# Attention's even-pair buffers over memory that the recurrence frees early, and a new order of the first loads and copies

## The chip, the cores and the metric

The kernel runs on one core of a Trainium2 chip. The metric is the device time of one execution in microseconds (us); the median of three runs is 3353.46 (3352.36 to 3354.02). Below, PE is TensorE (matrix multiplies), DVE is VectorE, ACT is ScalarE, POOL is GpSimd and SP is SyncE, which issues most of the transfers.

## What is computed

One layer over 2048 tokens of width 1024: a projection into many columns, a chunked attention branch, a recurrent branch, a gated merge, a residual, and a feed-forward network with a second residual.

```python
h   = RMSNorm_pre(x)
P   = h @ w_in            # q/k/v, r/k/v + low-rank w/a/g, branch gates
yA  = chunk-band attention (own chunk of 64 + 8 previous, bias on clipped distance)
yB  = RWKV-7 time mixing (token shift, decay, delta-rule state update over time)
m   = sigmoid(gA) * (yA @ proj_a) + sigmoid(gB) * (yB @ proj_b)
x   = x + RMSNorm_post(m @ w_out)
x   = x + RMSNorm_post2(relu(RMSNorm_pre2(x) @ w_up)^2 @ w_down)
```

## The kernel before, in words

**Arithmetic.** All products are of float32 precision made from three passes: each operand is split into a high part (a rounded copy, made by ACT) and a low part (the difference, made by DVE), and `mm3` (L78) multiplies high by high, high by low and low by high.

**Weights.** `wsplit` (L60 to L66) loads a block of 128 x 1024 (512 KB) into `wraw` from SP's queue, then ACT casts it into `whi` (L69) and DVE subtracts into `wlo` (L70). The pool `w` has two buffers of each, so the load of block n+2 waits for wlo of block n, and whi of block n+2 waits for the last matmul of block n. `dense` (L105) is one such block: 24 matmuls of 128 x 512 into `psd`.

**Stages.** The tokens are worked in four groups of 512. `phase_norm` (L313) makes the normed, transposed and split `hh`/`hl` of group 0: four tiles of 128 tokens, each loaded (x, L300), squared on ACT (L303), scaled on DVE with the broadcast gain g_pre (L306), and turned by PE (`pstr`, L144). Then each group runs

- `phase_rwkv`: dense blocks for the recurrence and the gates, and the recurrence of four pairs of heads, with `rwkv_pre` (L372) as the part ahead of each pair. `mix` (L325 to L329) takes a dense block's result, `lora` its low-rank parts, and E (L400) is the decay; X (L535) starts from x0, a pattern of ones spread over the partitions.
- `phase_attention`: four pairs (`att_pair`, L789). Each takes the old keys and values (KK, VV, L796 and L797) from memory, makes QA and QB from a dense block (L805 to L808; ACT and DVE in turn), then keys, values, scores and sums. `load_bias` (L902) reads the distance bias from `skew` in memory.
- `phase_merge`: four blocks of proj_b into md, four blocks of proj_a into th (`branches`, L961; the sum th + md, L978; its split into mh and ml, L69 and L70), then w_out in two halves (`ps_o`, L995), copied out by ACT (L1001). Beside it run the residual of the group before (o_prev L1024, transposed into `ps_ht` at L1030), and the norm of the next group (L300 to L306), or in the last group `combinations` (cmb, L1082) and the first operand of the feed-forward part (bh and bl, L1089 and L1090).

Then the feed-forward part runs in two halves.

**Constants.** `constants` (L150) is a generator. Its first part runs ahead of `phase_norm`, its second part behind: nine small loads into `rows` (L216), `raw2w` and `raw2a` (L223), `build_bias` (L236), which writes `band` (L896) and copies each of its eight rows of 768 over 128 partitions into `skew` (L898, eight transfers of 384 KB), and the x0 spread of eight transfers of 16 KB (L242).

**Order and memory.** A tile scheduler sets the order of the instructions on each engine; each engine then runs its own list in that order, with semaphores between them. Every pool is a stretch of SBUF; pools that open later reuse the addresses of pools that closed, and an instruction that writes there waits for the last users. Transfers from SP are also in order: one that waits holds back all behind it. In the attention, the pool `at` (two buffers, KK, VV, QA, QB among others) lies at 74400 to 135200 bytes of each partition and `atp` (PT, and the recurrence's output y) at 135200 to 176160.

Of the kernel before, what the change touches and what calls it, by code (L numbers as in the profile page):

```python
# [8 lines left out]
F32 = mybir.dt.float32  # L9
BF16 = mybir.dt.bfloat16  # L10
F32R = mybir.dt.float32r
# [6 lines left out]
P = 128  # L18
D = 1024
# [4 lines left out]
G = 512  # L24
GT = G // P
C = 64
# [14 lines left out]
RW0 = 1536  # L41
# [3 lines left out]
def advance(steps, n=None):  # L45

    while n is None or n > 0:
        if next(steps, steps) is steps:
            return
        n = n and n - 1  # L50


class Block:
# [3 lines left out]
        self.NG = self.S // G  # L57


    def wsplit(self, src, k, n):  # L60

        raw = self.wp.tile([P, k, n], F32, tag="raw", name="wraw")
        self.nc.sync.dma_start(raw, src)
        hi, lo = (self.wp.tile([P, k, n], F32R, tag="w" + x, name="w" + x) for x in ("hi", "lo"))
        self.split(hi, lo, raw)
        return hi, lo  # L66
# [41 lines left out]
    def dense(self, col):  # L108


        if self.g == 0:
            self.order.append(col)
            wh, wl = self.wsplit(*self.block(col))
        else:
            wh, wl = next(self.feed)
        ps = self.pd.tile([P, G], F32, tag="d", name="psd")
        self.mm = self.mm3(ps, [(wh[:, k], wl[:, k], self.h[0][:, k], self.h[1][:, k]) for k in range(KB)])
        return ps
# [31 lines left out]
    def constants(self, ctx, mixing):  # L150
        tc, nc, a = self.tc, self.nc, self.a
        keep = ctx.enter_context(tc.tile_pool(name="const", bufs=1))
        cp = mixing.enter_context(tc.tile_pool(name="mconst", bufs=1, side="right"))
        dp = ctx.enter_context(tc.tile_pool(name="scratch", bufs=1, space=DRAM))
# [50 lines left out]
        with tc.tile_pool(name="setup", bufs=1, side="right") as sp, \  # L205
             tc.tile_pool(name="setup_ps", bufs=1, space=PSUM, side="right") as pp:
            eye = sp.tile([2, 32, 16], F32, name="eye")
            nc.vector.memset(eye, 1.0)
            nc.gpsimd.affine_select(
                eye, eye, [[1, 32], [-2, 16]], ALU.is_equal, 0.0, base=0, channel_multiplier=-1  # L210
            )
            yield
            raw = sp.tile([nrow, P], F32, name="rows")
            at, off = 0, {}
            for name, n in rows:
                nc.sync.dma_start(raw[at : at + n], a[name].rearrange("(n p) -> n p", p=P))  # L216
                off[name] = at
                at += n
            raw2 = []
            for x in ("w2", "a2"):  # L220
                raw2.append(sp.tile([P, HW], F32, name="raw2"+x))
                for h in range(2):
                    nc.sync.dma_start(raw2[-1][h * C : h * C + C], a[x])  # L223
            ps = pp.tile([P, nrow], F32, name="ps_rows")
            nc.tensor.transpose(ps, raw, self.ident[:nrow, :nrow])
            nc.vector.tensor_copy(self.cst, ps)

            for par in range(2):
                r = slice(par * C, par * C + C)
                nc.scalar.copy(self.wh[par], raw2[par])  # L230
                o = slice(C - par * C, P - par * C)
                nc.vector.memset(self.wl[par][o].bitcast(F32), 0.0)
                nc.vector.tensor_tensor(
                    self.wl[par][r], raw2[par][r], self.wh[par][r].bitcast(F32), ALU.subtract
                )
            self.build_bias(sp, dp)  # L236
            eyeb = sp.tile([2, 512], BF16, name="eyeb")
            nc.vector.tensor_copy(eyeb, eye.rearrange("p r j -> p (r j)"))
            eyed = dp.tile([2, 512], BF16, name="eyed")
            nc.sync.dma_start(eyed, eyeb)  # L240
            for i in range(8):
                nc.sync.dma_start(  # L242
                    self.x0[i * 16 : i * 16 + 16].rearrange("p r j -> p (r j)"),
                    eyed[i % 2][None, :].to_broadcast((16, 512)),
                )

        def view(name, n):
            return self.cst[:, off[name] : off[name] + n]
# [44 lines left out]
        lo = self.hp.tile([P, KB, G], F32R, tag="hl", name="hl")  # L293
        return hi, lo

    def norm_steps(self, g, sp, pt, gt, t):

        nc = self.nc
        x = sp.tile([P, D], F32, tag="x", bufs=GT, name="x")
        nc.sync.dma_start(x, self.a["x"][g * G + t * P : g * G + (t + 1) * P])  # L300
        sq = sp.tile([P, D], F32, tag="sq", bufs=1, name="sqx")
        ssq = sp.tile([P, 1], F32, tag="ssq", bufs=4, name="ssq")
        nc.scalar.activation(sq, x, AF.Square, accum_out=ssq)  # L303
        r = self.rstd(sp, ssq, 1.0 / D, RMS_EPS)
        yield
        nc.vector.scalar_tensor_tensor(x, x, r, gt, op0=ALU.mult, op1=ALU.mult)  # L306
        yield
        if t == 0:
            self.h = self.alloc_h()
        self.transpose_split(pt, x, *self.h, slice(t * P, (t + 1) * P))  # L310
        yield

    def phase_norm(self, g, sp, pt):  # L313

        gt = self.gain(sp, self.a["pre_mix_g"], "g_pre")
        for t in range(GT):
            advance(self.norm_steps(g, sp, pt, gt, t))


    def mix(self, g, blk, out):  # L320
# [51 lines left out]
    def rwkv_pre(self, g, p, rp, NA, between=lambda: None):  # L372
        nc = self.nc
        pc = slice(p * P, (p + 1) * P)
        col = slice(p, p + 1)
# [8 lines left out]
        k = self.tmp("k")  # L384
# [5 lines left out]
        v = self.tmp("v")  # L390
        self.mix(g, 8 + p, v)

        between()
        nc.vector.tensor_scalar(tw, tw, -0.5 * DEC, -0.5 * DEC, ALU.mult, ALU.add)
        cum = tw
# [391 lines left out]


    def att_pair(self, g, p):  # L789
        nc, ap = self.nc, self.ap  # L790
        rows = [slice(0, C), slice(C, P)]
        first, lastg = g == 0, g == self.NG - 1
        KK = ap.tile([P, 2, 2, G], F32R, tag="KK", name="KK")
        VV = ap.tile([P, 2, GT, 2, C], F32, tag="VV", name="VV")
        if not first:
            nc.sync.dma_start(KK[:, :, 0].bitcast(F32), self.kc[p])  # L796
            nc.sync.dma_start(VV[:, 0], self.vc[p])  # L797
        bias = [self.load_bias(2 * p + par) for par in range(2)]

        ps = self.dense(ATT0 + p * P)  # L800
        QA = ap.tile([P, 2, G], F32R, tag="QA", name="QA")
        QB = ap.tile([P, 2, G], F32R, tag="QB", name="QB")
        for par in range(2):
            rw, ow = rows[par], rows[1 - par]
            nc.scalar.activation(QA[rw, par], ps[rw], AF.Copy, scale=-0.125)  # L805
# [79 lines left out]
    def build_bias(self, sp, dp):  # L885

        nc = self.nc

        self.skew = dp.tile([8, P * 769], F32, name="skew")
        band = dp.tile([8, 768], F32, name="band")  # L890
        ext = sp.tile([8, 768], F32, name="ext")
        nc.sync.dma_start(ext[:, 383:703], self.a["rel_rev"])
        nc.gpsimd.memset(ext[:, 703:768], 0.0)
        nc.vector.tensor_scalar(ext[:, 383:703], ext[:, 383:703], -1.0, None, ALU.mult)
        nc.vector.tensor_copy(ext[:, 0:383], ext[:, 383:384].to_broadcast((8, 383)))
        nc.sync.dma_start(band, ext)  # L896
        for h in range(8):
            nc.sync.dma_start(  # L898
                self.skew[h].rearrange("(q m) -> q m", m=769)[:, 0:768], band[h][None, :].to_broadcast((P, 768))
            )  # L900

    def load_bias(self, h):  # L902
        nc = self.nc
# [7 lines left out]
    def phase_attention(self, g):  # L911
        tc, nc = self.tc, self.nc
        self.yctx = ExitStack()
        yp = self.yctx.enter_context(tc.tile_pool(name="ya", bufs=1, side="right", reuse_waits="tile"))
        self.ya = self.alloc_y(yp)
        bp = self.yctx.enter_context(tc.tile_pool(name="br", bufs=1, side="right", reuse_waits="tile"))
        self.md = [bp.tile([P, 2, G], F32, name=f"md{i}") for i in range(KB // 2)]
        with ExitStack() as ctx:
            e = ctx.enter_context
            self.ap = e(tc.tile_pool(name="at", bufs=2, reuse_waits="tile"))  # L920
            pp = e(tc.tile_pool(name="atp", bufs=1, reuse_waits="tile"))
            self.psc = e(tc.tile_pool(name="atps", bufs=1, space=PSUM, reuse_waits="tile"))
            self.pt = e(tc.tile_pool(name="atpt", bufs=1, space=PSUM, reuse_waits="tile"))
            self.pv = e(tc.tile_pool(name="atpv", bufs=2, space=PSUM, reuse_waits="tile"))
            self.pts, self.npt = [], 0
            for i in range(2):
                self.pts.append([pp.tile([P, 6, 2 * P], F32, name=f"PT{par}{i}") for par in range(2)])
            for p in range(NP):
                self.att_pair(g, p)
                if p == 1:  # L930
                    for i in range(KB // 2):
                        self.load_gate(self.md[i], 1, i)
            y = self.load_y(pp, self.ap)
            for i in range(KB // 2):
                self.branches(y, self.md[i])
# [543 lines left out]
    def run(self):  # L1479
        tc, e = self.tc, None  # L1480
        with ExitStack() as ctx, ExitStack() as mixing:
            e = mixing.enter_context
            consts = self.constants(ctx, mixing)
            advance(consts, 1)
            self.pd = ctx.enter_context(tc.tile_pool(name="pd", bufs=2, space=PSUM))
            self.wp = e(tc.tile_pool(name="w", bufs=2))
            self.hp = e(tc.tile_pool(name="h", bufs=1))
# [82 lines left out]
```

## Time and profile before

| | |
|---|---|
| median of three runs | 3353.46 us |
| the profiled execution's own time | 3355.02 us |
| its span | 3353.1 us |
| PE busy | 3254.7 us, 97% |
| DVE busy | 2281.7 us, 68% |
| ACT busy | 1461.6 us, 44% |
| PE busy in the first 50 us | 29.19 us |

The span is what the profiler saw from the first to the last instruction. PE is at work for nearly all of it, so the idle time of PE is where to look; a wait of another engine costs only what PE waits for it. In the rows of a timeline, the first number is the start in us, the second the length, then engine, line, operation, output and inputs, count, and in brackets how long the engine had been idle and what released it. Rows of waits give the total in us, how many, and the longest.

### The profile page before, as it was taken

The numbers are of one execution on the slowest core, as the hardware profiler recorded it, in microseconds if no ns is written. First come the engines' busy times: TensorE is split into PE (matmuls) and PEld (weight loads), VectorE is DVE, ScalarE is ACT, GpSimd is POOL, SyncE is SP. The second block draws the span as 40 slices with busy tenths as digits, with TensorE's granted clock in tenths as the row PEclk, the third lists the DMA queues.
The fourth block names the chain that finished last, engine by engine and source line by source line (L and its number), as shares of the span: only waits on it lengthen the run. The fifth ranks groups of instructions, "written<-read, shape, count | busy, mean of one in ns | idle before, by whom it ended". The sixth has DMA issues, their size and how long they took to land. (4 is left out here: it accounts for less than half of the span.)

```text
span 3353.1 us, 49354 instructions
## 1 busy us (share of the span) xinstructions
PE 3254.7 (97%) x19089; PEld 2612.5 (78%) x19089; DVE 2281.7 (68%) x3806; ACT 1461.6 (44%) x2331; POOL 391.8 (12%) x732
## 2 busy tenths in 40 slices
PE   7999999999999999999999999999999999999998
PEld 5777777777777778777777777888887877888886
DVE  5774656675665774665774675876877777776778
ACT  3434634444644434644434644333331254454432
POOL 2110002110012210012210000111200011100002
PEclk9999999999999999999999999999999999999999
DMA  4224343125364224354224266334755364554443
GB/s 150 86 78 149 105 138 117 64 95 175 97 222 133 76 86 165 107 203 151 83 82 152 86 216 228 131 115 141 269 174 200 109 240 162 171 169 154 148 154 126
DMA packets 164945, 478.42 MB, mean 143 GB/s; under 512 B 17436, under 2 KB 34016, under 8 KB 162024
## 3 DMA queue, kind: packets, MB, share of 16 engines
q1 hardware_dynamic: 110120, 364.10, 33.3%
q0 software_dynamic: 18688, 63.98, 4.9%
q10 hardware_dynamic: 35904, 47.20, 3.9%
q8 instruction: 151, 2.47, 0.3%
q14 instruction: 82, 0.67, 0.1%
HBM read 355.64 MB, written 122.71 MB: 143 GB/s over the span
## 5 line engine op out<-in xcount | busy, mean ns | idle before, releaser
L78 PE MATMUL psd<-hh,whi 128*128 128x512 f32 x1344 | 545.2, 406 | 8.9 <-ACT whi L69 6.6
L78 PE MATMUL psd<-hl,whi 128*128 128x512 f32 x1344 | 541.6, 403 | 0.0
L78 PE MATMUL psd<-hh,wlo 128*128 128x512 f32 x1344 | 539.4, 401 | 0.6 <-DVE wlo L70 0.5
L69 ACT CAST whi<-wraw 128x1024 fp32r<-128x1024 f32 x232 | 243.5, 1050 | 530.7 <-PE psd L78 423.2
L78 PE MATMUL ps_dn<-fop 128*128 128x512 f32 x1920 | 440.7, 390 | 3.5 <-DVE u L1267 2.9
L70 DVE TENSOR_TENSOR wlo<-wraw,whi 128x1024 fp32r<-128x1024 f32 x232 | 283.0, 1220 | 213.5 <-ACT whi L69 193.8
L78 PEld LDWEIGHTS ps_dn<-fop 128*128 128x128 f32 x1920 | 359.0, 188 | 81.3 <-DVE u L1267 4.9
L78 PEld LDWEIGHTS psd<-hh,whi 128*128 128x128 f32 x1344 | 257.1, 191 | 65.1 <-ACT whi L69 7.4
L78 PEld LDWEIGHTS psd<-hh,wlo 128*128 128x128 f32 x1344 | 257.0, 191 | 56.6 <-issue 3.5
L78 PEld LDWEIGHTS psd<-hl,whi 128*128 128x128 f32 x1344 | 257.1, 191 | 51.3 <-issue 2.1
L78 PE MATMUL ps_dn<-fop,fop 128*128 128x512 f32 x1008 | 228.6, 389 | 0.0
L78 PEld LDWEIGHTS ps_dn<-fop,fop 128*128 128x128 f32 x1008 | 189.2, 188 | 39.3
L1267 DVE TENSOR_TENSOR u<-u,ps_dn 128x512 f32<-128x512 f32 x240 | 160.0, 682 | 51.9 <-PE ps_dn L78 51.2
L868 DVE CUSTOM_DVE_ANT_0 sc<-bias,ps_s 128x640 f32<-128x640 f32 (+4 forms) x128 | 94.1, 735 | 55.4 <-PE ps_s L862 47.1
L69 ACT CAST fop<-wdraw 128x1024 fp32r<-128x1024 f32 x40 | 41.9, 1047 | 191.4 <-DVE u L1267 106.9
L873 ACT ACTIVATE sc<-sc,mn 128x640 f32<-128x640 f32 (+4 forms) x128 | 97.8, 764 | 35.3 <-DVE mn L868 30.1
L69 ACT CAST s12h<-s 128x1024 fp32r<-128x1024 f32 x32 | 33.7, 1053 | 169.4 <-PE ps_u L78 164.6
L995 PE MATMUL ps_o<-whi,mh 128*128 128x512 f32 x256 | 102.6, 401 | 2.4 <-ACT o L1001 2.4
L995 PE MATMUL ps_o<-wlo,mh 128*128 128x512 f32 x256 | 102.3, 400 | 0.5 <-DVE wlo L70 0.4
L78 PE MATMUL ps_p<-yh,whi 128*128 128x512 f32 x256 | 101.9, 398 | 0.6 <-DVE th L961 0.6
L78 PE MATMUL ps_p<-yh,wlo 128*128 128x512 f32 x256 | 102.2, 399 | 0.0
L995 PE MATMUL ps_o<-whi,ml 128*128 128x512 f32 x256 | 101.7, 397 | 0.0
(378 smaller groups left out, 6751.1 us busy)
## 6 DMA issues: line engine op xcount, KB each, us to landing
wraw<-in_w_in_dram SPq DMA_DIRECT2D x168, 512.0 KB
wraw<-in_w_up_dram SPq DMA_DIRECT2D x80, 512.0 KB
ar<-sd SPq DMA_DIRECT2D x21, 1024.0 KB
wdraw<-in_w_down_dram SPq DMA_DIRECT2D x40, 512.0 KB
araw<-ad SPq DMA_DIRECT2D x40, 512.0 KB
gd<-gate ACTq DMA_DIRECT2D x64, 256.0 KB
wraw<-in_w_out_dram SPq DMA_DIRECT2D x32, 512.0 KB
ad<-r POOLq DMA_DIRECT2D x64, 256.0 KB, 2.7
```

The source lines that it names most:

```text
L69: self.nc.scalar.copy(hi, src)
L70: self.nc.vector.tensor_tensor(lo, src, hi.bitcast(F32), ALU.subtract)
L78: mm = nc.tensor.matmul(ps, l, r, start=start and n == 0, stop=stop and n == last).ins
L868: nc.vector.tensor_tensor_reduce(sc[:, 0:n], bias[:, s0:640], pss[:, c0 : c0 + n], 1.0, 3.0e38, ALU.add, ALU.min, mn,)
L873: nc.scalar.activation(sc[:, 0:n], sc[:, 0:n], AF.Exp, scale=-1.0, bias=mn, accum_out=sm)
L995: nc.tensor.matmul(ps[t], l[:, k, ts], r[:, k % 2], start=k == 0 and j == 0, stop=k == KB - 1 and j == 2)
L1267: nc.vector.tensor_tensor(u[t][:, ns], u[t][:, ns], ps, ALU.add)
```

## The change

**First transfers.** `wsplit` is cut into `wload` and `wparts`. `phase_norm` loads the four x first, then the gain, then the first two weight blocks, which it also splits; `dense` takes these from `self.first`. The nine `rows` loads go to ACT's queue, ahead of `phase_norm`. 

**Spreads.** The x0 spread and the skew copies become a generator, `spread`. `rwkv_pre` of group 0 takes eight steps of it in pair 0 (x0) and eight in pair 1 (skew), behind the weight load that was issued last.

**Attention.** KK, VV, QA and QB come from a pool of their own for each parity of the pair (`atq0`, `atq1`, one buffer each). The pools now open as `atp`, `at`, `atq1`, `atq0`: `atp` at 74400 to 115360, `at` at 115360 to 135200, `atq1` at 135200 to 155680, `atq0` at 155680 to 176160. Before, the first pair's KK lay over gC, n2, AR and SV of the recurrence; now the even pairs lie over E, mN, BK, NA, X, T and others, and the odd ones over the recurrence's temporaries.

```diff
+    def wload(self, src, k, n):
         raw = self.wp.tile([P, k, n], F32, tag="raw", name="wraw")
-        self.nc.sync.dma_start(raw, src)
+        self.loaded = self.nc.sync.dma_start(raw, src).ins
+        return raw, k, n
+
+    def wsplit(self, *block):
+        return self.wparts(*self.wload(*block))
+
+    def wparts(self, raw, k, n):
...
-            wh, wl = self.wsplit(*self.block(col))
+            wh, wl = self.first.pop(col, None) or self.wsplit(*self.block(col))
...
-            yield
             raw = sp.tile([nrow, P], F32, name="rows")
...
-                nc.sync.dma_start(raw[at : at + n], a[name].rearrange("(n p) -> n p", p=P))
+                nc.scalar.dma_start(raw[at : at + n], a[name].rearrange("(n p) -> n p", p=P))
...
+            yield
...
+        def spread():
             for i in range(8):
                 nc.sync.dma_start(
                     self.x0[i * 16 : i * 16 + 16].rearrange("p r j -> p (r j)"),
                     eyed[i % 2][None, :].to_broadcast((16, 512)),
                 )
+                yield
+            for h in range(8):
+                nc.sync.dma_start(
+                    self.skew[h].rearrange("(q m) -> q m", m=769)[:, 0:768], band[h][None, :].to_broadcast((P, 768))
+                )
+                yield
+
+        self.spread = spread()
...
+        xs = [self.norm_load(g, sp, t) for t in range(GT)]
         gt = self.gain(sp, self.a["pre_mix_g"], "g_pre")
+        first = [(col, self.wload(*self.block(col))) for col in (RW0 + 12 * P, RW0)]
         for t in range(GT):
-            advance(self.norm_steps(g, sp, pt, gt, t))
+            advance(self.norm_steps(g, sp, pt, gt, t, xs[t]))
+        for col, w in first:
+            self.first[col] = self.wparts(*w)
...
+        if g == 0 and p < 2:
+            with self.tc.issue_after(self.loaded):
+                advance(self.spread, 8)
...
-        nc, ap = self.nc, self.ap
+        nc, ap, aq = self.nc, self.ap, self.aq[p % 2]
...
-        KK = ap.tile([P, 2, 2, G], F32R, tag="KK", name="KK")
+        KK = aq.tile([P, 2, 2, G], F32R, tag="KK", name="KK")
...
+            pp = e(tc.tile_pool(name="atp", bufs=1, reuse_waits="tile"))
             self.ap = e(tc.tile_pool(name="at", bufs=2, reuse_waits="tile"))
-            pp = e(tc.tile_pool(name="atp", bufs=1, reuse_waits="tile"))
+            self.aq = [e(tc.tile_pool(name=f"atq{i}", bufs=1, reuse_waits="tile")) for i in (1, 0)][::-1]
```

VV, QA and QB change from `ap` to `aq` as KK does. The scheduler makes a new order from this. Three places:

SP's queue at the start, before, from the last of the small loads on (`x_104` is x0, in_w_in the weights, raw_1112 the loads of a later stage):

```order
L240 DMA eyed<-eyeb 2x512
L63 DMA wraw<-in_w_in_dram 128x1024 x2
L242 DMA x_104<-eyed 16x512 x3
L896 DMA band<-ext 8x768
L242 DMA x_104<-eyed 16x512 x4
L898 DMA skew<-band 128x768 x8
L242 DMA x_104<-eyed 16x512
L63 DMA wraw<-in_w_in_dram 128x1024 x11
L362 DMA raw_1112<-in_g_dram 128x512
```

and with the change:

```order
L245 DMA eyed<-eyeb 2x512
L62 DMA wraw<-in_w_in_dram 128x1024 x2
L249 DMA x_104<-eyed 16x512 x4
L923 DMA band<-ext 8x768
L249 DMA x_104<-eyed 16x512 x4
L62 DMA wraw<-in_w_in_dram 128x1024 x5
L255 DMA skew<-band 128x768 x8
L62 DMA wraw<-in_w_in_dram 128x1024 x4
L386 DMA raw_1112<-in_g_dram 128x512
```

The skew copies stood behind the second weight load; now they stand behind the ninth (two of the nine are ahead of these rows), and two loads go ahead of the x0 spread.

DVE in the last merge, from the second block of proj_a on, before (th_18801 is the first block's tile, th_18802 the second's; ps_p their product):

```order
L70 TENSOR_TENSOR wlo<-wraw,whi 128x1024
L961 SCALAR_TENSOR_TENSOR th_18802<-th_18802,ps_p 128x512
L70 TENSOR_TENSOR ml<-th_18801,mh 128x1024
L961 SCALAR_TENSOR_TENSOR th_18802<-th_18802,ps_p 128x512
L1082 TENSOR_TENSOR cmb<-cmb 128x512
L978 TENSOR_TENSOR th_18802<-th_18802,md_17329 128x1024
L70 TENSOR_TENSOR wlo<-wraw,whi 128x1024
L961 SCALAR_TENSOR_TENSOR th_18803<-th_18803,ps_p 128x512
L70 TENSOR_TENSOR ml<-th_18802,mh 128x1024
L1082 TENSOR_TENSOR cmb<-cmb 128x512
L961 SCALAR_TENSOR_TENSOR th_18803<-th_18803,ps_p 128x512
```

and with the change (th_18833, th_18834 and th_18835 are the first to third blocks):

```order
L75 TENSOR_TENSOR wlo<-wraw,whi 128x1024
L986 SCALAR_TENSOR_TENSOR th_18834<-th_18834,ps_p 128x512
L75 TENSOR_TENSOR ml<-th_18833,mh 128x1024
L1107 TENSOR_TENSOR cmb<-cmb 128x512
L986 SCALAR_TENSOR_TENSOR th_18834<-th_18834,ps_p 128x512
L1107 TENSOR_TENSOR cmb<-cmb 128x512
L1003 TENSOR_TENSOR th_18834<-th_18834,md_17353 128x1024
L1107 TENSOR_TENSOR cmb<-cmb 128x512 x3
L75 TENSOR_TENSOR ml<-th_18834,mh 128x1024
L1107 TENSOR_TENSOR cmb<-cmb 128x512
L986 SCALAR_TENSOR_TENSOR th_18835<-th_18835,ps_p 128x512
L1107 TENSOR_TENSOR cmb<-cmb 128x512
```

Before, eight of the cmb rows stood among proj_b's blocks above, and two among these rows; now none stands above, and seven among these rows.

ACT in the last merge, at the end of w_out's first half, before (o is the half's result, bh the first operand of the feed-forward part):

```order
L69 CAST s3h<-wraw 128x1024
L69 CAST whi<-wraw 128x1024 x2
L1089 CAST bh<-bl 128x1024
L1001 COPY o_18791<-ps_o 128x512
L1089 CAST bh<-bl 128x1024
L1001 COPY o_18792<-ps_o 128x512
L1001 COPY o_18793<-ps_o 128x512
L1001 COPY o_18794<-ps_o 128x512
L69 CAST whi<-wraw 128x1024
```

and with the change:

```order
L74 CAST s3h<-wraw 128x1024
L74 CAST whi<-wraw 128x1024
L1026 COPY o_18823<-ps_o 128x512
L1026 COPY o_18824<-ps_o 128x512
L1026 COPY o_18825<-ps_o 128x512
L1114 CAST bh<-bl 128x1024
L1026 COPY o_18826<-ps_o 128x512
L74 CAST whi<-wraw 128x1024
```

Before, a bh cast stood ahead of the first copy of ps_o and another ahead of the second; now three copies stand ahead of the first bh.

Two more places move that have no rows here: x of the next group's norm (L306) goes from among proj_b's blocks to those of proj_a and w_out in groups 0 to 2, and the transposes ps_ht of groups 1 and 2 stand about two matmuls later on PE.

More of the change, by code (lines that the diff above doesn't have):

```diff
@@ L57, in __init__ @@
         self.NG = self.S // G
-    def wsplit(self, src, k, n):
+    def wload(self, src, k, n):
         raw = self.wp.tile([P, k, n], F32, tag="raw", name="wraw")
-        self.nc.sync.dma_start(raw, src)
+        self.loaded = self.nc.sync.dma_start(raw, src).ins
[3 more added lines that the diff above has]
+    def wparts(self, raw, k, n):
         hi, lo = (self.wp.tile([P, k, n], F32R, tag="w" + x, name="w" + x) for x in ("hi", "lo"))
@@ L235, in constants @@
                 )
-            self.build_bias(sp, dp)
+            band = self.build_bias(sp, dp)
             eyeb = sp.tile([2, 512], BF16, name="eyeb")
@@ L294, in alloc_h, with norm_load, norm_steps @@
         return hi, lo
-    def norm_steps(self, g, sp, pt, gt, t):
+    def norm_load(self, g, sp, t):
+        x = sp.tile([P, D], F32, tag="x", bufs=GT, name="x")
+        self.nc.sync.dma_start(x, self.a["x"][g * G + t * P : g * G + (t + 1) * P])
+        return x
+    def norm_steps(self, g, sp, pt, gt, t, x=None):
         nc = self.nc
-        x = sp.tile([P, D], F32, tag="x", bufs=GT, name="x")
-        nc.sync.dma_start(x, self.a["x"][g * G + t * P : g * G + (t + 1) * P])
+        if x is None:
+            x = self.norm_load(g, sp, t)
         sq = sp.tile([P, D], F32, tag="sq", bufs=1, name="sqx")
@@ L789, in att_pair @@
     def att_pair(self, g, p):
-        nc, ap = self.nc, self.ap
+        nc, ap, aq = self.nc, self.ap, self.aq[p % 2]
         rows = [slice(0, C), slice(C, P)]
         first, lastg = g == 0, g == self.NG - 1
-        KK = ap.tile([P, 2, 2, G], F32R, tag="KK", name="KK")
-        VV = ap.tile([P, 2, GT, 2, C], F32, tag="VV", name="VV")
+        KK = aq.tile([P, 2, 2, G], F32R, tag="KK", name="KK")
+        VV = aq.tile([P, 2, GT, 2, C], F32, tag="VV", name="VV")
         if not first:
@@ L800, in att_pair @@
         ps = self.dense(ATT0 + p * P)
-        QA = ap.tile([P, 2, G], F32R, tag="QA", name="QA")
-        QB = ap.tile([P, 2, G], F32R, tag="QB", name="QB")
+        QA = aq.tile([P, 2, G], F32R, tag="QA", name="QA")
+        QB = aq.tile([P, 2, G], F32R, tag="QB", name="QB")
         for par in range(2):
@@ L896, in build_bias @@
         nc.sync.dma_start(band, ext)
[L897 to L900, printed above, removed]
+        return band
     def load_bias(self, h):
@@ L1484, in run @@
             advance(consts, 1)
+            self.first = {}
             self.pd = ctx.enter_context(tc.tile_pool(name="pd", bufs=2, space=PSUM))
```

## The prediction

> **What bounds the kernel now.** I read the page first. It has, as busy time, share of the span and count:
>
> ```profile
> PE 3254.7 (97%) x19089; PEld 2612.5 (78%) x19089; DVE 2281.7 (68%) x3806; ACT 1461.6 (44%) x2331; POOL 391.8 (12%) x732
> ```
>
> The span of this execution is 3353.1 us, so PE (TensorE) idles for 98.4 us of it. The change removes no matmul: it can only take from these 98.4 us, and from time in which PE runs at half clock. Next come PE's waits (us in total, times, longest):
>
> ```profile
> PE ps_t L569 <- DVE X L548: 26.6, 8, 3.8
> PE ps_ht L1030 <- DVE o_prev L1024: 7.6, 9, 1.1
> PE psd L78 <- ACT whi L69: 6.6, 2, 4.9
> PE ps_o L995 <- ACT o L1001: 2.4, 2, 1.9
> PE psd L78 <- DVE QA L808: 2.3, 4, 0.8
> ```
>
> The largest, in the recurrence, is not touched. The third is a weight block that comes late once, for 4.9 us; the fourth and fifth stand in the last merge and at the start of attention. Then the windows around that late block (us, then busy time and count of PE, PEld, DVE, ACT, POOL, then granted clock, DMA share, GB/s) and PE's timeline:
>
> ```profile
> 40.00:50.00 10.00, 6.00 (x13) 4.30 (x14) 4.87 (x6) 3.13 (x4) 0.97 (x2) 0.67 0.65 210
> 50.00:60.00 10.00, 10.00 (x45) 8.20 (x44) 4.19 (x5) 4.59 (x7) 1.73 (x4) 0.99 0.18 55
> ...
> 10.06 1.97 PE L144 MATMUL pstr<-ident,x 128*128 128x128 f32 x8 [10.06 <-DVE x L306]
> 23.44 0.79 PE L78 MATMUL psd<-hh,whi 128*128 128x512 f32 x1 [1.62 <-ACT whi L69]
> 25.20 0.80 PE L78 MATMUL psd<-hh,wlo 128*128 128x512 f32 x1 [0.54 <-DVE wlo L70]
> 43.96 0.79 PE L78 MATMUL psd<-hh,whi 128*128 128x512 f32 x1 [4.95 <-ACT whi L69]
> 50.38 0.39 PE L78 MATMUL psd<-hh,wlo 128*128 128x512 f32 x1
> ```
>
> PE starts at 10.06, its first dense block at 23.44, and it stands from 39.0 to 43.96. The clock in that window is 0.67: after the stall come 15 matmuls in 6.42 us (43.96 to 50.38), which at the pace of the window behind (45 in 10 us, 0.222 each) would take 3.4. Why the block is late, SyncE, VectorE and ScalarE show:
>
> ```profile
> 14.24 0.84 SPq L63 DMA_DIRECT2D wraw<-in_w_in_dram  x2
> 25.59 5.25 SPq L898 DMA_DIRECT2D skew<-band  x8
> 33.07 0.36 SPq L63 DMA_DIRECT2D wraw<-in_w_in_dram  x1
> ...
> 23.92 1.23 DVE L70 TENSOR_TENSOR wlo<-wraw,whi 128x1024 fp32r<-128x1024 f32 x1
> ...
> 41.82 0.63 ACT L400 ACTIVATE E<-tw 128x512 f32<-128x512 f32 x1 [1.90 <-DVE tw L396]
> 42.87 2.23 ACT L69 CAST whi<-wraw 128x1024 fp32r<-128x1024 f32 x2
> ```
>
> Buffer 1 of raw weights is free at 25.15 (end of wlo), but its next load is issued at 33.07, behind the eight skew copies, and its whi runs at 42.87, 17.3 us after the first skew issue. ScalarE's order holds it too: whi stands behind E.
>
> **The start, second stall.** Now the first two blocks load ahead of the constants and are split among the transposes; the third and fourth loads stand on SyncE ahead of the x0 spread, and whi of the third ahead of pr and lw on ScalarE. With wlo of the first ahead of the last hl (22.47 in the row further down), the third loads before 24 and, at the 512 KB that a load holds and the 210 GB/s of the window above, needs 2.5 us to move; block 2 ends at 39.0. The idle 4.95 goes and, as PE then runs through, the half-clocked stretch: 6.42 - 3.4 = 3.0. Together **-7.9** (bounds -8.2 and -5: only the idle time goes). Next late would be E's chain (41.82), but the blocks behind it have their raw data by then.
>
> The Trainium skill, "TensorE: Matmul & The Clock Gate", Part 1 (the HAM clock gate), has the clock halve after an idle window of about 3.4 us and come back after a busy one. The trace agrees in kind: after 4.95 us of idling the half-clocked stretch lasted 6.4 us. By that page's one window the loss would be an estimated 1.7 us instead of 3.0, and the sum 1.3 us smaller.
>
> **The start, first matmuls.** Before, and with the last step ahead of the first dense block:
>
> ```profile
> 0.80 0.40 SPq L134 DMA_DIRECT2D g_pre<-in_pre_mix_g_dram  x1
> 1.25 1.94 SPq L300 DMA_DIRECT2D x<-in_x_dram  x4
> ...
> 8.72 1.28 DVE L306 SCALAR_TENSOR_TENSOR x<-x,rs_r,g_pre 128x1024 f32<-128x1024 f32 x1 [3.33 <-POOL rs_r L125]
> 22.47 0.69 DVE L147 TENSOR_TENSOR hl<-pstr,hh 128x512 fp32r<-128x512 f32 x1 [0.16 <-ACT hh L146]
> ```
>
> Now g_pre stands behind the four x (the third waits for the first to land, g_pre for the second), and ScalarE issues nine small loads ahead of its first square. So the first L306 may start up to 2.2 us later. Against that, the wlo that PE waited for at 25.20 lie ahead of the last hl, so the gaps between 23.44 and 25.20 shrink (1.76 us for two matmuls that are 0.43 us apart later in this spell: 0.9). I take **-1.0**, bounds -2.5 and +2.
>
> **The skew copies, later.** They stand now behind the ninth weight load, and the tenth behind them:
>
> ```profile
> 68.83 28.97 SPq L63 DMA_DIRECT2D wraw<-in_w_in_dram  x5
> ...
> 89.20 1.05 ACT L69 CAST whi<-wraw 128x1024 fp32r<-128x1024 f32 x1 [0.70 <-PE psd L78]
> ```
>
> The ninth was issued at 68.83, now about 8 earlier: 60.8. If whi of the tenth can run 17.3 us after the first skew issue, as before, that is 78.1; it was wanted at 89.20, now 81.2. So they are hidden with 3 us to spare: **0**, bounds 0 and +8 (the whole second stall again).
>
> The Trainium skill, "DMA: Bandwidth & Descriptors", section "Issuing engines are not separate DMA queues", says that all issuing engines share the same 16 DMA engines. This speaks against the change: the copies' traffic is moved, not lost, and the nine loads on ScalarE save SyncE's issue time alone; by it the gain rests on where the copies land.
>
> **Attention's buffers.** One dense block's queries are evacuated by ScalarE and VectorE in turn:
>
> ```profile
> 799.04 0.59 ACT L805 ACTIVATE QA<-psd 64x512 fp32r<-64x512 f32 x1
> 804.50 0.47 PE L78 MATMUL psd<-hh,whi 128*128 128x512 f32 x1 [0.50 <-DVE QA L808]
> ```
>
> QA's write follows its block at once, and PE's gap waits for QA's evacuation out of PSUM, not for a buffer of keys or values. New addresses change neither. **0**, bounds -2.3 (all of that wait) and 0.
>
> **Merges of groups 1 and 2.** With `atp` lower, x of the next norm lies over attention's outputs, and L306 moves from proj_b into proj_a. VectorE there:
>
> ```profile
> 952.80 1.28 DVE L306 SCALAR_TENSOR_TENSOR x<-x,rs_r,g_pre 128x1024 f32<-128x1024 f32 x1 [0.83 <-POOL rs_r L125]
> 954.01 1.28 DVE L961 SCALAR_TENSOR_TENSOR th<-th,ps_p 128x512 f32<-128x512 f32 x2
> 956.55 1.22 DVE L978 TENSOR_TENSOR th<-th,md 128x1024 f32<-128x1024 f32 x1
> 964.32 1.22 DVE L70 TENSOR_TENSOR ml<-th,mh 128x1024 fp32r<-128x1024 f32 x1
> 995.14 1.06 PE L1030 MATMUL ps_ht<-ident,o_prev 128*128 128x128 f32 x8 [0.89 <-DVE o_prev L1024]
> ```
>
> A proj_a block costs VectorE one wlo (1.23), two L961 (1.28), L978 (1.22) and ml (1.22): 5.0 us, beside 24 matmuls of 0.227, 5.45 us, on PE. One L306 makes it 6.2; blocks without one give it back. PE's transposes ps_ht stand about two matmuls later, so each of a group's four waits (0.89 here) can shrink by up to 0.45, 1.8 a group; but x comes later too. I take one wait's worth in each group: **-0.9**, bounds -3.6 and +2. Group 0 has no ps_ht: 0.
>
> **The last merge.**
>
> ```profile
> 1985.82 0.69 DVE L1082 TENSOR_TENSOR cmb<-cmb 128x512 f32<-128x512 f32 x1 [1.15 <-DMA cmb<-ht]
> ...
> 2019.47 1.04 ACT L1089 CAST bh<-bl 128x1024 fp32r<-128x1024 f32 x1 [6.03 <-DMA bl<-ht]
> 2021.05 0.50 PE L995 MATMUL ps_o<-whi,mh 128*128 128x512 f32 x1 [1.90 <-ACT o L1001]
> 2023.42 0.63 PE L995 MATMUL ps_o<-whi,mh 128*128 128x512 f32 x1
> 2026.40 0.46 PE L995 MATMUL ps_o<-wlo,mh 128*128 128x512 f32 x1
> ```
>
> Eight of the 16 cmb stood among proj_b's blocks; now all stand from the second block of proj_a on. Two blocks there now hold eight cmb (5.5), four L961 (2.6), two ml, two wlo and one L978 (6.1): 14.2 us against 10.9 on PE, 3.3 over. How much shows depends on slack; between 0 and 3.3 I take half, +1.7. On ScalarE three o copies go ahead of bh, which waited for its data and held them: PE's 2.4 goes. The half clock behind it (eight starts, 2.98 us from 2023.42 to 2026.40, for 1.6: 1.4) I don't count, as the new wait may bring a like spell. **-0.7**, bounds -3.8 and +5.
>
> **Sum.** -7.9 - 1.0 - 0.9 - 0.7 = -10.5 us. The profiled execution took 3355.02 us, 1.6 above the median of 3353.46; differences carry over, so 3343.0 us. A measurement of this kernel can tell about 0.2% from no change, 6.7 us: faster is below 3346.8, slower above 3360.2.
>
> **The rivals.** (a) Slower: VectorE sets proj_a's pace in all merges. Groups 0 to 2 pay 4 x 0.8 each, 9.6; the last has four cmb a block, 5.0 + 2.8 - 5.45 = 2.3, in four blocks 9.2; with four half-clocked spells of 1.4 that is +24.4, less 8.9 of the start: +15.5, **3369**. It decides if the evacuation of ps_p falls behind by more than the bank in hand (half a block, 2.7 us) and nothing in w_out catches up. For it: the order. Against: wlo runs ahead today, and L306 is one per block. Chance 0.06. (b) The skew copies stall block 10 as they stalled block 3: the 7.9 comes back, -2.6, **3351**, if they take over 20.4 us instead of 17.3; DMA share behind 50 us is 0.18 against 0.65, which speaks against it. 0.09. (c) The last merge loses its upper bound, +5 instead of -0.7: **3349**. 0.12. (d) The relocation does what it is said to, and PE's wait for QA goes: -2.3, **3341**. 0.07. That it brings nothing is in my forecast.
>
> **The numbers.** The forecast itself, 0.66, spans 3339 to 3348 by the start's bounds; nine tenths of it are faster. Faster: 0.59 + (d) 0.07 + a third of (c), 0.04 = 0.70; same: 0.07 + (b) 0.09 + the rest of (c), 0.08 = 0.24; slower: (a), 0.06. The range reaches down to (d) with the lower ends of the merges, 3338, and up to (b), 3351; (a) and the far ends stay out.
>
> **What would show it.** Right: PE runs through from its first dense block to 60 us with no wait for whi over 1 us and one half-clocked spell, not two; ps_o's 2.4 us wait is gone; QA's 2.3 us is still there. Wrong: a wait for whi near 80 us behind skew; PE waiting for th or wlo in proj_a by more than 5 us in all; a first dense block later than 25 us.

## The result and the profile after

The changed kernel takes 3344.35 us in the median of 18 runs (3339.09 to 3351.48), the kernel before beside it 3352.73 (18 runs, 3349.40 to 3355.44). The ratio is 0.9978, 95% interval 0.9972 to 0.9985: 7.4 us less, 5.0 to 9.4. The forecast was 3343.0, which was 10.5 us under the 3353.46 that stood as the median of the kernel before. The profiled execution of the changed kernel took 3343.45 us, its span is 3341.4.

Page of the changed kernel, busy time by engine, and PE's waits (us in total, times, longest):

```profile
PE 3247.1 (97%) x19089; PEld 2609.7 (78%) x19089; DVE 2280.8 (68%) x3806; ACT 1461.0 (44%) x2331; POOL 398.3 (12%) x732
...
PE ps_t L596 <- DVE X L575: 26.7, 8, 3.9
PE pstr L149 <- DVE x L326: 5.8, 1, 5.8
PE ps_ht L1055 <- DVE o_prev L1049: 4.9, 6, 1.1
PE ps_o L1020 <- DVE wlo L75: 4.9, 3, 3.6
PE psd L83 <- DVE QA L835: 2.3, 4, 0.8
PE ps_p L83 <- DVE th L986: 1.2, 1, 1.2
```

The wait of psd for whi (6.6) is gone, and so is that of ps_o for ACT's o (2.4). The wait for QA stands at 2.3 as before. ps_o now waits 4.9 us for wlo, where it waited 0.4; 3.6 of these come at once. The start of the program, by windows and on PE's timeline:

```profile
40.00:50.00 10.00, 10.00 (x46) 8.21 (x45) 7.28 (x9) 4.69 (x8) 3.16 (x6) 1.00 0.33 104
50.00:60.00 10.00, 10.00 (x50) 8.42 (x49) 6.45 (x11) 5.59 (x8) 2.48 (x6) 1.00 0.24 82
...
25.54 1.22 PE L83 MATMUL psd<-hh,whi 128*128 128x512 f32 x2
29.54 0.63 PE L83 MATMUL psd<-hh,wlo 128*128 128x512 f32 x1
29.97 0.44 PE L83 MATMUL psd<-hh,whi 128*128 128x512 f32 x1
69.86 1.13 PE L533 MATMUL ps_A<-AR,BK 64*128 64x128 f32 x8 [0.64 <-DVE BR L549]
```

From 40 to 50 us PE is busy for all 10.00 us at a clock of 1.00; before, it was busy for 6.00 at 0.67. The first dense block starts later, at 25.54 instead of 23.44. In the kernel before, the ps_A of the recurrence that waits for BR stands here:

```profile
77.14 1.13 PE L506 MATMUL ps_A<-AR,BK 64*128 64x128 f32 x8 [0.64 <-DVE BR L522]
```

So the start has gained 7.28 us by then, 2.10 less than the 9.38 gained between the first dense block and this ps_A. Why the first block is later, SyncE (its issues, then its waits) and VectorE show, and the last transposes on PE, before and after:

```profile
0.80 5.93 SPq L313 DMA_DIRECT2D x<-in_x_dram  x4
6.78 0.43 SPq L139 DMA_DIRECT2D g_pre<-in_pre_mix_g_dram  x1
...
SPq L313 <- DMA x<-in_x_dram: 3.3, 1, 3.3
SPq L313 <- DMA rows<-in_a_dram: 1.1, 1, 1.1
...
13.80 3.68 DVE L326 SCALAR_TENSOR_TENSOR x<-x,rs_r,g_pre 128x1024 f32<-128x1024 f32 x3 [2.97 <-DMA g_pre<-in_pre_mix_g_dram]
...
19.85 1.97 PE L144 MATMUL pstr<-ident,x 128*128 128x128 f32 x8 [0.70 <-DVE hl L147]
23.75 1.97 PE L149 MATMUL pstr<-ident,x 128*128 128x128 f32 x8 [0.55 <-DVE hl L152]
```

Issuing the four x takes 5.93 us instead of 1.94, since one of them waits 3.3 us for the first x to land and another 1.1 us for one of the small loads that ScalarE issued. So g_pre is issued at 6.78 instead of 0.80, and L326 (L306 before) waits for it until 13.80, where it started at 8.72. Of these 5.1 us the last transposes still show 3.9, because three L326 then run back to back, and the first dense block shows 2.1, because it no longer waits 1.62 us for its whi as it did at 23.44. In the last merge VectorE and PE read:

```profile
1991.11 0.69 DVE L1107 TENSOR_TENSOR cmb<-cmb 128x512 f32<-128x512 f32 x1 [2.99 <-DMA cmb<-ht]
1993.40 0.69 DVE L1107 TENSOR_TENSOR cmb<-cmb 128x512 f32<-128x512 f32 x1 [1.00 <-DMA cmb<-ht]
1995.75 1.22 DVE L75 TENSOR_TENSOR wlo<-wraw,whi 128x1024 fp32r<-128x1024 f32 x1
...
1997.02 0.80 PE L1020 MATMUL ps_o<-wlo,mh 128*128 128x512 f32 x1 [3.56 <-DVE wlo L75]
...
1997.00:2004.00 7.00, 6.98 (x19) 5.51 (x20) 6.56 (x8) 1.30 (x2) 0.71 (x1) 0.57 0.93 301
```

VectorE does not run out of time here: it sits idle, first for 2.99 us and then for 1.00, at a cmb whose data has not landed, while th, the sum and wlo stand behind it in its list. PE then waits 3.56 us for that wlo, and its granted clock in the 7 us behind is 0.57: 14 starts, from 1997.02 to 2002.74, are 0.43 apart but for the ends, where 0.23 is the full pace.

A table of starts, each read from the first matmul of its kind in the profiled execution, as the difference to the kernel before (whose own starts or lengths stand in the first row, us). "First 20 steps" is the time from the first start of the first dense block to the 21st, and "behind them" from there to the first ps_A:

| kernel | first dense block | first 20 steps | behind them | first ps_A | merges of groups 1 and 2, together | last merge, proj_b to ps_u |
|---|---|---|---|---|---|---|
| before | 23.44 | 8.12 | 41.75 | 73.30 | 312.1 | 109.9 |
| changed | +2.1 | -1.3 | -8.1 | -7.3 | -2.9 | +3.1 |
| e1, start alone | +1.8 | -2.8 | -8.1 | -9.0 | +4.7 | 0.0 |
| e2, pools alone | -0.6 | +0.2 | 0.0 | -0.4 | -2.5 | +3.7 |
| e3, skew early | +2.4 | -2.2 | -7.4 | -7.2 | -1.8 | +3.9 |
| e4, gain first | -1.0 | -0.7 | -7.9 | -9.6 | -2.8 | +2.7 |
| e5, spreads alone | +0.3 | +0.7 | -7.9 | -6.9 | +3.4 | +0.3 |
| e6, preload alone | +2.5 | -3.1 | -7.0 | -7.7 | -2.2 | +4.6 |
| e7, last pools | -0.8 | -1.5 | -7.9 | -10.2 | -2.7 | +3.0 |
| e8, cmb in w_out | +2.5 | -1.5 | -8.1 | -7.1 | -0.3 | -2.5 |
| e9, gain first and cmb in w_out | -1.1 | -0.4 | -7.8 | -9.3 | -1.6 | -0.3 |

A merge here runs from the first matmul of proj_b to the next group's first ps_A; the last one from proj_b to the first ps_u of the feed-forward part. Each is one execution, and not always a typical one: that of e1 (3352.98) and that of e5 (3352.42) are the slowest of their 11, that of e2 (3351.10) the fastest. Parts that a kernel does not touch differ by a few us too: from ps_u to the end the changed kernel's profile is 4.9 us shorter than before's, and the other nine are 1.3 to 3.9 shorter. So of the 11.6 us between the two profiled executions, that stretch is no effect of the change. What several kernels show alike is safer than one row: the stretch behind the first 20 steps is 7.0 to 8.1 shorter in all nine kernels whose third and fourth loads go ahead of the skew copies, and unchanged in e2. The merges of groups 1 and 2 take 309.2 to 311.8 us in the eight kernels with the new pools and 312.1 to 316.9 in the three without.

### The profile page after: what moved, and what is told of

The parts are those of the page before. It is cut to its first block, busy times and chain, and to the rows that moved or that the text cites. A ratio compares the mean times of both kernels' runs of the same rounds, so it can differ in the third digit from the quotient of the medians.

```text
span 3341.4 us, 49351 instructions
## 1 busy us (share of the span) xinstructions
PE 3247.1 (97%) x19089; PEld 2609.7 (78%) x19089; DVE 2280.8 (68%) x3806; ACT 1461.0 (44%) x2331; POOL 398.3 (12%) x732
```

## The experiments

**e1 and e2: the two halves of the change.** e1 has the new start and the old attention pools, e2 the reverse.

```diff
 # e1, against the changed kernel
-        KK = aq.tile([P, 2, 2, G], F32R, tag="KK", name="KK")
+        KK = ap.tile([P, 2, 2, G], F32R, tag="KK", name="KK")
...
-            pp = e(tc.tile_pool(name="atp", bufs=1, reuse_waits="tile"))
             self.ap = e(tc.tile_pool(name="at", bufs=2, reuse_waits="tile"))
-            self.aq = [e(tc.tile_pool(name=f"atq{i}", bufs=1, reuse_waits="tile")) for i in (1, 0)][::-1]
+            pp = e(tc.tile_pool(name="atp", bufs=1, reuse_waits="tile"))
```

In e1 VV, QA and QB go back to `ap` too; e2 makes the opposite edit in the kernel before.

> The new start and spreads with the attention pools of before. Theory: the gain is the start's, 7.3 us in the two profiles (ps_A at 77.14 before, 69.86 after), and the pools cost about 2 us (merges of groups 1 and 2 -1.1, last merge +3.2). So about 3345.4 us, 7.3 under the kernel before, and in its trace the last merge as before (wait of ps_o for ACT o 2.4 us, none for wlo). Rival: the pools bring the 3 us by which the median's 8.4 exceed 7.3 - 2 = 5.3; then start alone gains 5 at most, about 3347.5 or more.

> The new attention pools with the start and spreads of before. Theory: slower by about 2 us, 3354.8 (merges of groups 1 and 2 -1.1, last merge +3.2, with the 3.6 us wait of ps_o for wlo back in its trace), attention's wait for QA unchanged at 2.3 us. Rival: the pools gain about 3 us, 3349.7.

Measured: e1 3343.98 against 3353.42, ratio 0.9977 (0.9968 to 0.9985); e2 3354.18, ratio 1.0005 (0.9996 to 1.0014). The start alone gives what the whole change gives, and the pools alone cost between -1.3 and +4.7 us. The rival, a gain of 3 us by the pools, lies outside e2's interval. PE's waits of e2:

```profile
PE psd L78 <- ACT whi L69: 6.6, 2, 5.0
PE ps_o L996 <- DVE wlo L70: 5.7, 3, 4.3
PE psd L78 <- DVE QA L808: 2.3, 4, 0.8
```

The second stall is back, the wait for wlo in the last merge came with the pools, and QA's wait does not care for them. In the table the pools show as about -2.5 in the merges of groups 1 and 2 and +3.7 in the last, a sum of about +1 from one execution.

**e3: the skew copies early.**

```diff
-        if g == 0 and p < 2:
+        if g == 0 and p == 0:
             with self.tc.issue_after(self.loaded):
-                advance(self.spread, 8)
+                advance(self.spread, 16)
```

> As changed, but the skew copies are issued in pair 0, right behind the x0 spread and ahead of the fifth weight load. Theory A (the copies' place makes the gain): the fifth block waits as the third did before, 5 us of idling and up to 3 of half clock: 5 to 8 us over the changed kernel, 3350 to 3352. Theory B (it is the two loads ahead that make it): the copies start near 31.3 and free the queue about 17 us later, near 48.6, where the fifth block is wanted near 50; no wait, the time of the changed kernel within 1 us.

Measured: 3347.76 against 3353.42, ratio 0.9979 (0.9970 to 0.9988), as the changed kernel's 0.9978, and ps_A at 7.2 us earlier than before, as there. Theory B holds. SyncE and ScalarE of e3:

```profile
23.46 2.87 SPq L62 DMA_DIRECT2D wraw<-in_w_in_dram  x2
31.57 5.15 SPq L255 DMA_DIRECT2D skew<-band  x8
37.41 31.20 SPq L62 DMA_DIRECT2D wraw<-in_w_in_dram  x6
...
48.82 1.05 ACT L74 CAST whi<-wraw 128x1024 fp32r<-128x1024 f32 x1 [2.54 <-DMA wraw<-in_w_in_dram]
```

The fifth block's whi ran 17.25 us after the first skew issue, as the third's did in the kernel before (17.3), and it did wait for its data. But it is wanted only then: PE lost 0.36 us at that block, to wlo, and the stretch behind the first 20 steps is 0.7 longer than in the changed kernel.

**e4: the gain first.**

```diff
-        xs = [self.norm_load(g, sp, t) for t in range(GT)]
         gt = self.gain(sp, self.a["pre_mix_g"], "g_pre")
+        xs = [self.norm_load(g, sp, t) for t in range(GT)]
...
-                nc.scalar.dma_start(raw[at : at + n], a[name].rearrange("(n p) -> n p", p=P))
+                nc.sync.dma_start(raw[at : at + n], a[name].rearrange("(n p) -> n p", p=P))
```

The `yield` of `constants` goes back ahead of these loads, as in the kernel before.

> As changed, but g_pre is loaded ahead of the four x, and the nine small loads go back to SyncE's queue behind the first two weight blocks. Theory: in the changed kernel the first scaling L306 waits until 13.80 for g_pre and starts 5.1 later than before (8.72), of which the first dense block shows 2.1 (25.54 against 23.44). With g_pre first it starts by 10 and the first dense block by 23: 2 to 3 us under the changed kernel, about 3341.9. Rival: the small loads, ahead of the constants that VectorE makes, and the transposes of x set the start; then the first dense block stays at 25 and the time is unchanged.

Measured: 3343.58, ratio 0.9974 (0.9964 to 0.9984). VectorE and PE of e4:

```profile
8.79 1.28 DVE L326 SCALAR_TENSOR_TENSOR x<-x,rs_r,g_pre 128x1024 f32<-128x1024 f32 x1 [3.41 <-POOL rs_r L130]
...
22.40 1.22 PE L83 MATMUL psd<-hh,whi 128*128 128x512 f32 x2 [0.68 <-ACT hh L151]
```

L326 starts at 8.79 and the first dense block at 22.40, 3.1 earlier than in the changed kernel; ps_A comes 2.4 earlier (table). The times' intervals overlap, so the gain is shown by the trace and not by the medians. The run undoes two things at once, the gain behind the x and the small loads on ScalarE; which of them held the x was not tried apart.

**e5 and e6: the spreads alone, the preload alone.** e5 is the kernel before with the generator `spread` and its two calls in `rwkv_pre`; e6 is the changed kernel with the spreads done at once.

```diff
 # e6, against the changed kernel
-        self.spread = spread()
+        advance(spread())
...
-        if g == 0 and p < 2:
-            with self.tc.issue_after(self.loaded):
-                advance(self.spread, 8)
```

> The kernel before, with only the x0 spread and the skew copies moved into the generator; first transfers and pools as before. In its SyncE queue the third and fourth weight loads stand ahead of x0 and skew. Theory: the second stall comes from the third load standing behind the skew copies, so this alone takes the wait of psd for whi (4.95) and its half clock: ps_A 7 to 9 us earlier than before, 3345. Rival: ScalarE's order (whi of the third behind E) holds it by itself, and without the preloaded blocks the stall stays: 3353.

> As changed, but the x0 spread and the skew copies stay in the constants; the first two blocks are still loaded ahead. In its SyncE queue x0 stands ahead of the third and fourth weight loads, and skew behind them. Theory (what counts is that the third and fourth loads go ahead of the skew copies, by whichever edit): no wait of psd for whi, ps_A 7 to 9 us earlier than before, about 3345. Rival (the copies must go behind the ninth load): the fifth or sixth block waits for 2 us or more and the time is 3348 or above.

Measured: e5 3346.52 against 3354.35, ratio 0.9978 (0.9969 to 0.9986); e6 3350.74 against 3356.10, ratio 0.9984 (0.9975 to 0.9993). Each brings the start forward by itself, ps_A by 6.9 and 7.7 us. SyncE and ScalarE of e5, and behind them DMA share and GB/s (the last two figures) of the kernel before while its third block was missing:

```profile
25.44 1.46 SPq L63 DMA_DIRECT2D wraw<-in_w_in_dram  x2
27.00 4.77 SPq L244 DMA_DIRECT2D x<-eyed  x8
62.30 7.18 SPq L250 DMA_DIRECT2D skew<-band  x8
...
33.44 1.05 ACT L69 CAST whi<-wraw 128x1024 fp32r<-128x1024 f32 x1 [8.84 <-PE psd L78]
...
41.00:42.00 1.00, 0.00 (x0) 0.00 (x0) 0.79 (x1) 0.18 (x1) 0.00 (x0) 1.00 1.01 332
42.00:43.00 1.00, 0.00 (x0) 0.00 (x0) 0.52 (x1) 1.00 (x3) 0.49 (x1) 1.00 0.88 360
43.00:44.00 1.00, 0.04 (x1) 0.04 (x1) 0.24 (x2) 0.91 (x1) 0.23 (x1) 0.70 0.10 41
```

What they share is that the third and fourth loads go ahead of the skew copies. In e5 whi of the third also comes ahead of E on ScalarE (33.44, where it ran at 42.87 before), so the load and ScalarE's order were freed together. The rows of the kernel before tell how much of its 4.95 us each held. Its third and fourth loads were both on their way, 1.05 MB, and the transfers stop soon after 43; at these 332 to 360 GB/s they take about 3 us, so by this estimate the third block's data was complete at about 41.7 at the earliest (of the 4096-byte packets that make up the two loads, the trace has the 128th of 256 end at 41.82). ScalarE started whi at 42.87. So the load alone held the block for about 3.9 of the 4.95 us or more, and ScalarE's order for about 1 at most.

For e6 the rival was right in part: the fifth block waits for its load, 2.68 us on ScalarE at 48.39. PE felt 0.49 of it directly, and the stretch behind the first 20 steps is 1.0 longer than in the changed kernel. Its 3350.74 lies above the 3348 that the rival named, but beside a kernel before that ran at 3356.10; a gain of 5.4 us (2.3 to 8.4) does not tell theory from rival. The trace does: there is no stall like the old one.

**e7: cmb's buffers free early again.** As e4, with the pools of the last group opened in the order at, atq1, atq0, atp.

```diff
+            if g < self.NG - 1:
+                pp, self.ap = pool("atp", 1), pool("at", 2)
+                self.aq = [pool(f"atq{i}", 1) for i in (1, 0)][::-1]
+            else:
+                self.ap, self.aq = pool("at", 2), [pool(f"atq{i}", 1) for i in (1, 0)][::-1]
+                pp = pool("atp", 1)
```

> As e4 (g_pre first, small loads back on SyncE), but in the last group the pools open in the order at, atq1, atq0, atp, so that cmb's buffers come free before proj_b as they did before. Theory: the last merge's loss is the cmb rows behind transfers that start late, as their buffers lie over y; with them among proj_b's blocks again the wait of ps_o for wlo (4.9 us) goes and the last merge takes what it took before, 3.3 us less than in the changed kernel: 3.3 under e4, about 3340.3. Rival: the sum of VectorE's work is what binds, wherever cmb stands; then within 1 us of e4.

Measured: 3354.64, ratio 1.0003 (0.9994 to 1.0012), about 10 us over e4, against both theory and rival. The trace names two new waits. ScalarE and PE at the start of the last group's attention:

```profile
1817.40 0.59 ACT L833 ACTIVATE QB<-psd 64x512 fp32r<-64x512 f32 x1 [4.25 <-DMA yd<-yf]
1819.51 0.38 PE L889 MATMUL ps_s<-KK,QA 128*128 128x320 f32 x1 [2.27 <-ACT yh L74]
1822.22 0.76 PE L83 MATMUL psd<-hh,whi 128*128 128x512 f32 x1 [2.18 <-DVE QA L835]
```

By the allocated addresses QB of the first pair (131104 to 135200) now lies over the recurrence's yf (134080 to 136128), and waits 4.25 us for the store that still reads it; PE idles for 2.27 and 2.18 us, and the granted clock is 0.93 and 0.90 in the two stretches of 20 us from 1804 on. The attention of this group is 7.4 us longer than in the kernel before (from ps_s to proj_b). In the merge, th's transfers are behind a cmb transfer that waits for its buffer, in VectorE's words:

```profile
1977.09 1.28 DVE L990 SCALAR_TENSOR_TENSOR th<-th,ps_p 128x512 f32<-128x512 f32 x2 [5.11 <-DMA th<-gd]
```

So the expectation fell: cmb stood among proj_b's blocks again, and a transfer held VectorE elsewhere. What e7 does show is that the place of the first pair's buffers can cost several us; in the kernel before it cost none.

**e8 and e9: cmb behind proj_a.** e8 is the changed kernel with one line changed, e9 is e4 with the same line.

```diff
-                    self.phase_merge(g, o, self.after(g, sp, pt), early)
+                    self.phase_merge(g, o, self.after(g, sp, pt) if g < self.NG - 1 else early)
```

> As changed, but combinations is stepped in w_out's first half instead of behind each proj_a block of the last merge. Theory: VectorE waits 3.0 and 1.0 us for cmb's data ahead of th and wlo (at 1991.11 and 1993.40 in the changed kernel), and PE 3.6 us for that wlo; with cmb behind them these waits go, and the o copies stay ahead of bh, so that neither the 3.6 nor the old 2.4 is left: the last merge 5 us shorter than in the changed kernel, about 3339.5. Rival: the cmb then hold the low parts at the start of the feed-forward part, and the time comes back there.

> e4 and e8 together. Theory: the two gains lie in different places and add: 2 from the start, 5 from the last merge, about 3337.5. Rival: as for e8.

Measured: e8 3344.36 against 3354.35, ratio 0.9967 (0.9956 to 0.9979); e9 3342.47, ratio 0.9963 (0.9949 to 0.9977). VectorE's wait for cmb in the last merge, 1925 to 2050 us, of the changed kernel and then of e8:

```profile
DVE cmb L1107 <- DMA cmb<-ht: 4.0, 2, 3.0
```

```profile
DVE cmb L1107 <- DMA cmb<-ht: 9.1, 2, 8.0
...
2014.47 0.69 DVE L1107 TENSOR_TENSOR cmb<-cmb 128x512 f32<-128x512 f32 x1 [7.98 <-DMA cmb<-ht]
2016.35 0.50 PE L1020 MATMUL ps_o<-wlo,mh 128*128 128x512 f32 x1 [1.15 <-DVE wlo L75]
2016.00:2023.00 7.00, 6.01 (x24) 4.42 (x24) 5.60 (x9) 1.52 (x2) 1.32 (x2) 1.00 1.01 369
...
PE ps_o L1020 <- DVE wlo L75: 3.2, 4, 1.1
```

The waits for cmb's data do not go in e8, against its theory: they are longer, 9.1 us instead of 4.0. But the long one now comes at 2014.47, when th and the sums have long been made, and PE feels 1.15 us of it instead of 3.56. The longest wait of PE for wlo is 1.1 us, over all merges, and its clock stays at 1.00 behind it. The last merge is 5.6 us shorter than in the changed kernel, 3.4 in e9; the five kernels with these pools and cmb behind proj_a's blocks (the changed kernel, e2, e3, e4, e6) all lie between +2.7 and +4.6, so this is clear of what one execution may differ by. From ps_u to the end e8 and e9 are 3.8 and 2.2 us shorter than before's profile, as the others are, so nothing came back there. The times do not show it: both run under the changed kernel's ratio of 0.9978, e9 at 12.4 us under the kernel before (7.7 to 17.1), but the intervals overlap.

## Why the prediction was right, step by step

The forecast gain of 10.5 us lies outside the measured 5.0 to 9.4. The time itself came within 1.4 us of the forecast partly by luck, as the kernel before ran at 3352.73 beside it and not at 3353.46. By terms:

- **Second stall**, -7.9 forecast, bounds -8.2 and -5: right in place and in size. From the 21st start of the first dense block to the first ps_A 8.1 us went: the idle 4.95 and the half-paced spell behind it. (The 15 starts of that spell are 14 steps, so at 0.227 us a step it had cost 3.2 us and not 3.0.) An estimate by the one window of the Trainium skill, "TensorE: Matmul & The Clock Gate", Part 1, put the gain 1.3 us lower; the trace does not agree, with 6.4 us of half pace in the kernel before and the 8.1 us that went.
- **First matmuls**, -1.0 forecast, bounds -2.5 and +2: the net is +0.8, and one step failed. It said that the first L306 may start up to 2.2 us later; it was 5.1. The prediction had g_pre wait only for the second x to land, but its issue stood behind all four x at 6.78, and it landed just ahead of 13.80. So the first dense block came 2.1 later, at 25.54, which is past the 25 us that the prediction named as a sign of being wrong. e4 puts it right. The gaps, 0.9 forecast, shrank by 0.7 (the third start comes 1.02 behind the first instead of 1.76). Another 0.6 of the first 20 steps is a shorter slow spell, and that is luck: the table has these steps anywhere from 3.1 shorter to 0.7 longer.
- **Skew copies**, 0 forecast: right. In the changed kernel the tenth block's whi ran at 81.91, and 81.2 was the time at which it was said to be wanted; it waited for PE, not for its data:

```profile
61.92 6.89 SPq L255 DMA_DIRECT2D skew<-band  x8
...
81.91 1.05 ACT L74 CAST whi<-wraw 128x1024 fp32r<-128x1024 f32 x1 [0.70 <-PE psd L83]
```

  Rival (b) needed more than 20.4 us for the copies; e3 measured 17.25. The copies took their time wherever they stood, as the prediction reckoned; it was hidden. The sentence of the Trainium skill, "DMA: Bandwidth & Descriptors", section "Issuing engines are not separate DMA queues", was not tested by this, since SyncE issues the copies in every run.
- **Attention's buffers**, 0 forecast: right, and rival (d) is out, QA's 2.3 us are there in the changed kernel and in e2. No wait of PE over 0.8 us stands in the attention of the kernel before, so there was little to lose; e7 shows what a wait for a buffer looks like.
- **Merges of groups 1 and 2**, -0.9 forecast, bounds -3.6 and +2: -2.9 in the changed kernel, -0.3 to -2.8 in the other kernels with these pools. The waits that the term was made of, ps_ht's for o_prev, fell from 7.6 to 4.9 us.
- **Last merge**, -0.7 forecast, bounds -3.8 and +5: +3.1; this step failed too. The gain named, ps_o's 2.4 us behind bh, came. The loss was larger, nearer to rival (c), and of another kind: not VectorE's sum of work but its list standing still at a cmb whose data had not landed. e8 puts the same wait where less hangs on it, and the loss goes. The place was wrong as well: the prediction put it into proj_a, and PE felt it at a wlo of w_out's first half. The half-paced spell behind the new wait, which the prediction left out of the sum against the old one of 1.4 us, cost 2.8 (13 steps of 0.44 on average instead of 0.227).
- **Rival (a)** did not come about: PE's waits for th are 1.2 us in all. The rest of what was named as a sign of being right is there: no wait for whi, one half-paced spell up to 60 us, ps_o's 2.4 us gone, QA's 2.3 left.

The terms as measured, -8.1 and +0.8 at the start, -2.9 and +3.1 from the merges, make -7.1, beside -7.4 by the runs. With stretches that differ by a few us from one execution to the next, so close an agreement is in part luck. The sum of 10.5 was too large by the two steps that failed, 1.8 and 3.8 us, less the 2.0 and 0.2 that the merges and the stall gave above their forecast.

## What to carry to other kernels

When the first transfers are reordered, read who waits for the last of them: a small operand moved behind large ones can hold the whole start. A large copy costs little where it stands behind enough loads of the next work: here two loads ahead of it took the stall from 8.1 us to 1.0 or less. When pools move, list what will lie over their old and new places in every later stage, for an instruction that waits for its data at the head of an in-order list holds everything behind it, however idle its engine is. Such a wait need not be removed; it is enough to put it where little hangs on it.

## What the runs showed of the hardware

Between 20 and 30 us the granted clock reads 1.00 in both kernels, though the first matmuls after the transposes are 0.43 us apart (26.55, 26.98, 27.41, and so on to 29.97) and 0.23 from then on. The clock's record does not show this first slow spell; the spacing does. Its length differs from kernel to kernel: the first 20 steps take 5.0 us in e6, 6.8 in the changed kernel and 8.8 in e5, where 20 steps of 0.227 are 4.5.

The skew copies held the weight load behind them for 17.3, 17.25 and 17.4 us (kernel before, e3, e6), counted from the first issue to the whi of that load; in the kernel before up to about 1 us of it may be ScalarE's order.

The changed kernel scatters more than the kernel before: 12.4 us from lowest to highest of 18 runs against 6.0. So does e1, 13.9 in 11 runs against 8.6 in the 30 beside it, but not e3 (7.2 in 11 against 8.6 in 30) nor e6 (7.9 in 11 against 10.5 in 14), so it does not go with the new start as such. In the 18 runs the time falls with the mean granted clock, by 1.8 us for each 0.001 (correlation -0.76, from 3351.48 at 0.990 to 3339.09 at 0.995). What makes the clock vary was not tried.
